# Threshold attention on one core: first keys rounded from PSUM, 20 exponential buffers, a new order table and one more GpSimd drain

## The chip, the core and the metric

The kernel runs on one core of one Trainium2 chip. The metric is the device time of one execution in microseconds (us), the median of several runs. Five engines work in their own instruction queues: TensorE (PE: matmuls and transposes), VectorE (DVE), ScalarE (ACT), GpSimd (POOL) and SyncE (SP, which issues transfers). A matmul writes to PSUM, and here only ACT and DVE empty PSUM. "The granted clock" is TensorE's, as a share of full speed.

## What is computed

For each of 96 heads (batch 8 by 12 heads), with Q, K and V of 512 rows by 64 in float32:

```python
scores  = einsum('bhqd,bhkd->bhqk', Q, K) / 8
weights = softmax(scores)                      # over the keys
weights = where(weights > 0.1, weights, 0)
weights = weights / (sum(weights) + 1e-10)
out     = einsum('bhqk,bhkd->bhqd', weights, V)
```

With normally distributed inputs almost no softmax weight is over 0.1, so nearly all rows of the output are zero.

## The kernel before

It uses that. Approximate weights in fp16 are computed for everything, only to find the few rows of Q in which a weight may pass the threshold. Those rows are gathered, scored again in float32, and their results are scattered into an output that is filled with zeros meanwhile. A check at the end (line 769 loads one number, `many`) branches to an exact fallback, which isn't taken here.

**Tiling.** Two heads are a pair, two pairs a quad: 48 pairs in 24 quads. A pair's scores are made in 4 score steps of 128 keys, each for both heads, so there are 192 score steps and 384 exponentials of 128 by 512. Quads 0 and 1 are brought in by single pairs, so that work can start sooner.

**What is done for a quad.** `load_k` and `load_q` (lines 330, 334) bring K in two 128 KB transfers per pair, one for each head, and Q. `do_ktr` (381) transposes K on PE in float32 into two PSUM banks, half the keys in each. `do_kev` (389 on ACT, 391 on DVE) copies each bank to SBUF in float32 (`kt`, which the later rescoring reads). `do_kh` (396 on ACT, 400 on GpSimd) casts `kt` to fp16 for the scores. `do_qcast` (367, 371) casts Q to fp16, `do_qtr` transposes it, and `do_qev` (416) copies that to SBUF. `do_sc` (438) makes the scores of one step, in two PSUM banks. `do_ex` takes an exponential from one bank into an fp16 buffer `e`: ACT by its function (447), DVE by arithmetic on the number's bits (449). `do_sm` (468) sums them and their eighth powers over the keys on PE. `do_bits` (425 GpSimd, 427 ACT, 429 DVE) makes the squares, or on DVE a bound of them, of the fp16 keys and queries of a quad, in two steps (a = 0 queries, a = 1 keys), and `do_norms` (478) adds them up on PE in an accumulator of their own, 4 matmuls for a quad; the maximum of these norms (`do_nm`, 491) bounds the error of fp16 and goes into the check.

**The chain behind.** The pairs form three groups (24, 16 and 8 pairs). For a group, when its sums are complete: `y` (the threshold, 483 ff.), `d`, `fl`, `mx` (candidate rows). Then for each of 6 stages of 8 pairs: `m`, `ix`, `qi`, `qf` (row numbers; 513, 524, 529), `gq` (GpSimd gathers rows of Q, 534), `xm` and `xev` (547), `xqk` (rescoring in float32 on PE, 556), `xexp` (ACT, 562), `xcut`, `xkeep` (DVE, 566, 570), `vi`, `oi` (575, 580), `gv` (GpSimd gathers rows of V, 585) and `scatter` (GpSimd, 600). The last group has one stage, number 5. The output's zeros are 24 transfers of 512 KB on SP's queue (607).

**What sets the order.** Each of these steps is added to a plan with its dependencies and the buffers that it takes and gives back. A table `ORDER`, one word for a step, lists them all in one sequence: the word's digits (base 36) are the step's number, its letter the engine (P, V, A, G for PE, DVE, ACT, GpSimd; S and Q for loads issued by SP and by ACT; N for none). The steps are emitted in that sequence, and each engine works through its own in that order. Buffers come from rings, first freed first used: 7 PSUM banks (`one`), 32 SBUF buffers of 512 KB for loads, `kt`, fp16 operands and squares (`big`), 14 for exponentials (`e`). A load waits on its queue until the buffer that the sequence gives it is free. `behind` and `alone` keep certain GpSimd and DVE steps from running at once. Constants are steps too: `const_base` (23 short DVE instructions, up to line 265) is needed first by the index step `qi`.

## Time and profile before

| | |
|---|---|
| median of 3 runs | 174.43 us (173.22, 174.43, 174.43) |
| the profiled execution | 173.78 us |
| its span, first to last instruction | 172.0 us |
| PE busy | 160.1 us (93%), 2190 instructions |
| DVE busy | 150.1 us (87%), 349 |
| ACT busy | 149.4 us (87%), 297 |
| POOL (GpSimd) busy | 130.4 us (76%), 198 |
| mean granted clock | 0.994 |

Busy times are sums over the whole span; a busy PE is not PE at its peak, since its matmuls are pipelined and their ends are modelled. Idle time of an engine that nobody waits for costs nothing. The single rows read from the trace stand in a section of their own below.

### The profile page before, as it was taken

The numbers are of one execution on the slowest core, as the hardware profiler recorded it, in microseconds if no ns is written. First come the engines' busy times: TensorE is split into PE (matmuls) and PEld (weight loads), VectorE is DVE, ScalarE is ACT, GpSimd is POOL, SyncE is SP. The second block draws the span as 40 slices with busy tenths as digits, with TensorE's granted clock in tenths as the row PEclk, the third lists the DMA queues.
The fourth block names the chain that finished last, engine by engine and source line by source line (L and its number), as shares of the span: only waits on it lengthen the run. The fifth ranks groups of instructions, "written<-read, shape, count | busy, mean of one in ns | idle before, by whom it ended". The sixth has DMA issues, their size and how long they took to land. (4 is left out here: it accounts for less than half of the span.)

```text
span 172.0 us, 5811 instructions
## 1 busy us (share of the span) xinstructions
PE 160.1 (93%) x2190; PEld 62.7 (36%) x2190; DVE 150.1 (87%) x349; ACT 149.4 (87%) x297; POOL 130.4 (76%) x198
## 2 busy tenths in 40 slices
PE   6598999999999999999999999999999999998950
PEld 2253443443354243434442354334243333332320
DVE  5198999999999999999999999899689999997450
ACT  2577999999999999999999999999899999936720
POOL 8119979999989988960785999799869959536451
PEclk9999999999999999999999999999999999999997
DMA  5999999989899689796998989999899980000000
GB/s 162 263 234 286 238 268 252 278 194 270 184 269 289 143 235 379 166 326 150 226 331 243 320 185 264 360 385 266 268 308 374 398 346 13 1 3 5 6 5 7
DMA packets 67453, 38.27 MB, mean 222 GB/s; under 512 B 51938, under 2 KB 64349, under 8 KB 67424
## 3 DMA queue, kind: packets, MB, share of 16 engines
q1 hardware_dynamic: 64992, 37.10, 76.1%
q10 hardware_dynamic: 1856, 0.66, 1.6%
q8 instruction: 17, 0.28, 0.7%
q0 software_dynamic: 576, 0.13, 0.5%
q14 instruction: 12, 0.10, 0.2%
HBM read 25.56 MB, written 12.78 MB: 223 GB/s over the span
## 5 line engine op out<-in xcount | busy, mean ns | idle before, releaser
L447 ACT ACTIVATE e<-one 128x512 f16<-128x512 f32 x231 | 120.0, 639 | 3.2 <-PE one L438 2.2
L449 DVE TENSOR_SCALAR e<-one 128x512 uint16<-128x512 f32 x153 | 97.0, 683 | 3.3 <-PE one L438 2.9
L438 PE MATMUL one<-big 64*128 64x512 f16 x384 | 67.6, 391 | 1.0 <-ACT big L396 0.5
L468 PE MATMUL sum<-e,w_s 128*32 128x512 f16 (+1 forms) x768 | 59.4, 387 | 0.9 <-ACT e L447 0.7
L425 POOL TENSOR_TENSOR big<-big 128x512 bf16<-128x512 f16 x52 | 52.8, 1038 | 2.3 <-DVE big L429 1.8
L400 POOL CAST big<-big 128x512 f16<-128x512 f32 x47 | 28.2, 613 | 16.3 <-ACT big L389 4.5
L371 POOL CAST qh<-big 128x512 f16<-128x512 f32 x45 | 26.7, 614 | 6.0 <-DMA big<-in_Q_dram 3.0
L438 PEld LDWEIGHTS <-big 64*128 64x128 f16 x384 | 17.2, 97 | 34.5 <-issue 28.1
L468 PEld LDWEIGHTS <-w_s 128*32 128x32 f16 (+1 forms) x768 | 15.9, 95 | 36.1 <-issue 31.5
L389 ACT COPY big<-one 128x512 f32<-128x512 f32 (+1 forms) x37 | 20.5, 591 | 2.7 <-PE one L381 2.6
L416 DVE COPY big<-one 128x512 f16<-128x512 f16 (+1 forms) x52 | 19.5, 398 | 3.3 <-PE one L410 1.2
L381 PE MATMUL one<-identity_f,big 64*128 64x64 f32 x384 | 18.7, 234 | 1.7 <-DMA big<-in_K_dram 1.5
L381 PEld LDWEIGHTS one<-identity_f,big 64*128 64x128 f32 x384 | 16.1, 145 | 6.9 <-issue 3.0
L391 DVE COPY big<-one 128x512 f32<-128x512 f32 (+1 forms) x15 | 9.7, 649 | 3.6 <-PE one L381 3.4
L556 PE MATMUL one<-big,xq 128*32 128x512 f32 x96 | 11.5, 598 | 0.5 <-issue 0.5
L410 PEld LDWEIGHTS <-qh 64*128 64x128 f16 x384 | 9.0, 97 | 7.6 <-issue 3.5
L410 PE MATMUL one<-identity_h,qh 64*128 64x64 f16 x384 | 11.3, 195 | 0.0
L534 POOL DMA_INDIRECT qs<-in_Q_dram,idx x6 | 6.4, 1060 | 6.2 <-DVE idx L524 4.8
L600 POOL DMA_INDIRECT out_dram<-vr,idx x6 | 6.1, 1024 | 4.1 <-DVE cut L566 2.2
L427 ACT ACTIVATE big<-big 128x1024 bf16<-128x1024 f16 x8 | 8.3, 1059 | 0.0
L585 POOL DMA_INDIRECT vr<-in_V_dram,idx x6 | 6.4, 1066 | 2.3 <-DVE idx L575 1.3
L562 ACT ACTIVATE one<-one 128x512 f32<-128x512 f32 x6 | 3.7, 612 | 3.3 <-DVE vals L504 2.0
(83 smaller groups left out, 80.9 us busy)
## 6 DMA issues: line engine op xcount, KB each, us to landing
out_dram<-zero SPq DMA_DIRECT2D x24, 512.0 KB, 6.2
big<-in_K_dram SPq DMA_DIRECT2D x93, 128.0 KB, 4.2
big<-in_Q_dram SPq DMA_DIRECT2D x22, 512.0 KB, 5.5
big<-in_Q_dram SPq DMA_DIRECT2D x3, 256.0 KB
big<-in_K_dram ACTq DMA_DIRECT2D x3, 128.0 KB
big<-in_Q_dram ACTq DMA_DIRECT2D x1, 256.0 KB
qs<-in_Q_dram,idx POOLq DMA_INDIRECT x6
vr<-in_V_dram,idx POOLq DMA_INDIRECT x6, 4.0
```

Of the source, the lines that this page charges most:

```text
L371: behind(nc.gpsimd.tensor_copy(dst, src))
L381: nc.tensor.matmul(dst[i][:, c:c + D], lhsT=src[ps, n0 + n, r, :], rhs=identity_f32[ps, ps], is_transpose=True, start=True, stop=True)
L389: nc.scalar.copy(dst, src)
L400: behind(nc.gpsimd.tensor_copy(dst, src))
L410: nc.tensor.matmul(dst[i][:, c:c + D], lhsT=src[ps, n0 + n, r, :], rhs=identity_h[ps, ps], is_transpose=True, start=True, stop=True)
L416: nc.vector.tensor_copy(qk_b[big("qk", q)][:, 0, n0:n0 + k, i * SO * D:(i + 1) * SO * D], src)
L425: behind(nc.gpsimd.tensor_tensor(out=dst[:, n, :], in0=src[:, n, :], in1=src[:, n, :], op=ALU.mult))
L438: nc.tensor.matmul(one[at("one", ("sc", hp, t, h))][:], lhsT=qk[ps, 1, n, t * P:(t + 1) * P], rhs=qk[ps, 0, n, :], start=True, stop=True)
L447: nc.scalar.activation(dst, src, ACTF.Exp, scale=scale, bias=-11.0 * math.log(2.0))
L449: nc.vector.tensor_scalar(dst.bitcast(u16), src, scale * LOG2E * 1024.0, 4096.0, op0=ALU.mult, op1=ALU.add)
L468: nc.tensor.matmul(dst[32 * j:32 * j + 32, :], lhsT=w, rhs=x, start=first, stop=False, skip_group_check=True)
L556: nc.tensor.matmul(one[at("one", ("xs", x))][sl, :], lhsT=xq_b[at("xq", x)][:, n, sl], rhs=kt_b[big("kt", quads[j])][:, n, :], start=(n == ...
```

## The change

1. A new step `kx` for the first unit (pair 0, `units[0]`): each half of its transposed K is rounded from its PSUM bank straight to the fp16 operand, on ACT or DVE. `kh` of that pair is gone. The float32 copies (`kev`) are still made, after `kx` in each bank. The score steps of pair 0 wait only for the half that holds their 128 keys (`t // 2`).
2. The ring `e` has 20 buffers, not 14.
3. `ORDER` is a new table (1327 words, 1325 before), so all queues have a new order and many steps are on another engine.
4. One `nc.gpsimd.drain()` is added as a step behind the last group's `mx`; the last scatter comes after it.
5. In the branch that isn't taken, two loads go to ACT's queue.

```diff
-ORDER = """6N fQ hS 1G gQ 24S 7P 18Q 22S 8P 9P 0G 5V 23S ...
+ORDER = """0G fS hQ iV 6N 4G 7P 8P 9P aP bP cP dP gQ jP ...
-    pools = {"one": 7, "sum": 1, "big": 32, "qh": 2, "e": 14,
+    pools = {"one": 7, "sum": 1, "big": 32, "qh": 2, "e": 20,
...
+    def do_kx(eng, u, i):
+        q, n, _ = u
+        src = one[at("one", ("ktr", u, i))][:, 0:SO * D]
+        dst = qk_b[big("qk", q)][:, 1, n, i * SO * D:(i + 1) * SO * D]
+        if eng == "ACT":
+            nc.scalar.copy(dst, src)
+        else:
+            nc.vector.tensor_copy(dst, src)
...
+        split = u == units[0]
+        for i in range(2) if split else ():
+            add(("kx", u, i), {"ACT": 0.27, "DVE": 0.33}, 0.15, [("ktr", u)], g0 - 9,
+                lambda e, u=u, i=i: do_kx(e, u, i), takes=[("big", ("qk", q))] if i == 0 else [])
         for i in range(2):
             add(("kev", u, i), {"ACT": 0.055 + 0.207 * k, "DVE": 0.062 + 0.267 * k}, 0.15,
-                [("ktr", u)] + [("kev", w, 0) for w in prev] + [("kev", u, 0)] * i, g0 - 9,
+                [("ktr", u)] + [("kx", u, i)] * split + [("kev", w, 0) for w in prev] + [("kev", u, 0)] * i, g0 - 9,
...
-        for n in range(n0, n0 + k):
+        for n in range(n0, n0 + k) if not split else ():
...
-                add(("sc", hp, t), {"PE": 0.22}, 0.23, [("qev", u, 0), ("qev", u, 1), ("kh", q, n)], g - 3,
+                add(("sc", hp, t), {"PE": 0.22}, 0.23, [("qev", u, 0), ("qev", u, 1)] + ([("kx", u, t // 2)] if split else [("kh", q, n)]), g - 3,
...
-            xstep("scatter", {"POOL": 1.25}, 0.3, ["gv", "oi"] + [("z", j) for j in quads_of(x)], do_scatter)
+            xstep("scatter", {"POOL": 1.25}, 0.3, ["gv", "oi"] + [("z", j) for j in quads_of(x)]
+                  + [("drain", 0)] * (x == NX - 1), do_scatter)
+    add(("drain", 0), {"POOL": 1.95}, 0.0, [("mx", NG - 1)], 999, lambda e: nc.gpsimd.drain())
```

**What the new table moves, counted.** Steps on each engine up to its last exponential, and the squarings (bits) behind it:

| | ACT before | ACT now | DVE before | DVE now |
|---|---|---|---|---|
| exponentials | 231 | 238 | 153 | 146 |
| K evictions, full (two pairs) | 31 | 28 | 13 | 16 |
| K evictions, half (one pair) | 6 | 3 | 2 | 5 |
| `kx` | - | 2 | - | 0 |
| `kh` casts | 1 | 2 | 0 | 0 |
| `qcast` casts | 2 | 0 | 1 | 1 |
| `y` | 1 | 0 | 1 | 2 |
| index steps `qi`, `qf` | - | - | 7 | 10 |
| `const_base` | - | - | at the very start | at about the 211th exponential |
| bits | 2 | 0 | 9 | 4 |
| bits behind the last exponential | 6 | 8 | 5 | 15 |

DVE's cast of Q is that of quad 1's second pair before, and of the very first pair now, ahead of all other work on data. GpSimd has 21 bit steps (26 before), 45 casts of K (47), 47 of Q (45), and the drain, which stands behind the last `gq` and ahead of the last three `gv`. `const_base` stands behind work of the full stretch now.

**The loads at the start.** Before, ACT's queue had both head halves of K of pair 0, Q of pair 1 and one half of K of pair 1, and SP's had Q of pair 0, Q of quad 1's first pair, then the rest. Now SP issues the first half of K of pair 0, then K of quad 1's first pair, its Q, K of pair 1 and the others; ACT issues Q of pair 0 and then the second half of K of pair 0.

**The loads late in the order.** The K of quad 20 now takes a buffer that the first rescoring (stage 0) gives back, 10 score steps ahead of its transposes, and the four transfers of K of quad 21 stand just ahead of it on SP's queue. Q of quad 12 has a buffer that comes free 10 score steps ahead too (by the casts of quad 11). In the old table the shortest such distance was 8 score steps (K of quad 17), and the next 16 and more.

ACT's queue at its start, before: names are buffers (`big` the large ring, `qh` the cast of Q, `one` a PSUM bank, `e` an exponential).

```order
L330 DMA big0_114<-in_K_dram 128x4x64 x2
L334 DMA big1_115<-in_Q_dram 128x2x256
L330 DMA big0_114<-in_K_dram 128x4x64
L367 ACT_TABLE_LOAD
L367 CAST qh0_146<-big1_115 128x512
L389 COPY big4_118<-one1_107 128x256
L396 CAST big5_119<-big4_118 128x512
L367 CAST qh1_147<-big2_116 128x512
L447 ACTIVATE e1_149<-one1_107 128x512
```

And the same place now, where the lines 407 and 456 are `kx` and the exponential:

```order
L334 DMA big1_115<-in_Q_dram 128x2x256
L330 DMA big0_114<-in_K_dram 128x4x64
L407 ACT_TABLE_LOAD
L407 CAST big2_116<-one1_107 128x256
L407 CAST big2_116<-one2_108 128x256
L456 ACTIVATE e0_148<-one6_112 128x512
L456 ACTIVATE e0_148<-one5_111 128x512
L456 ACTIVATE e1_149<-one3_109 128x512
```

Two of four load issues, two casts of Q, the half eviction and the cast behind it have left ACT's head; the two halves of K come from the PSUM banks `one1` and `one2`, and exponentials follow at once.

ACT's queue from its last exponential on, before (427 squarings, 547 `xev`, 562 the exponential of the rescoring):

```order
L447 ACTIVATE e8_156<-one0_106 128x512
L427 ACTIVATE big10_124<-big16_130 128x1024
L547 COPY xq1_187<-one1_107 128x256
L562 ACTIVATE one3_109,cut3_191<-one3_109 128x512
L547 COPY xq0_186<-one6_112 128x256
L427 ACTIVATE big7_121<-big29_143 128x1024 x2
L547 COPY xq1_187<-one3_109 128x256
L562 ACTIVATE one1_107,cut4_192<-one1_107 128x512
L427 ACTIVATE big24_138<-big4_118 128x1024
L562 ACTIVATE one6_112,cut5_193<-one6_112 128x512
L427 ACTIVATE big17_131<-big6_120 128x1024
L427 ACTIVATE big21_135<-big2_116 128x1024
```

And now, from behind the first rescoring of the tail on (436 squarings, 556 `xev`, 571 the exponential of the rescoring):

```order
L571 ACTIVATE one6_112,cut3_197<-one6_112 128x512
L436 ACTIVATE big10_124<-big13_127 128x1024
L571 ACTIVATE one1_107,cut4_198<-one1_107 128x512
L556 COPY xq1_193<-one4_110 128x256
L571 ACTIVATE one5_111,cut5_199<-one5_111 128x512
L436 ACTIVATE big29_143<-big16_130 128x1024
L436 ACTIVATE big4_118<-big30_144 128x1024
L436 ACTIVATE big28_142<-big26_140 128x1024
L436 ACTIVATE big11_125<-big0_114 128x1024
L436 ACTIVATE big9_123<-big1_115 128x1024
```

Five squarings now stand behind the last rescoring exponential (`cut5`), where two stood.

DVE's queue behind the rescoring exponential of stage 4, before (429 bits, 566 `xcut`, 570 `xkeep`, 575 `vi`):

```order
L429 TENSOR_SCALAR big24_138<-big4_118 128x512
L566 TENSOR_SCALAR cut4_192<-cut4_192 128x1
L570 SCALAR_TENSOR_TENSOR junk_200,accs_98<-one1_107,cut4_192,key_no_93 128x512
L575 TENSOR_SCALAR idx4_178<-accs_98,base_96 128x1
L566 TENSOR_SCALAR cut5_193<-cut5_193 128x1
L570 SCALAR_TENSOR_TENSOR junk_200,accs_98<-one6_112,cut5_193,key_no_93 128x512
L575 TENSOR_SCALAR idx5_179<-accs_98,base_96 128x1
```

And now (438 bits, 575 `xcut`, 579 `xkeep`, 584 `vi`):

```order
L575 TENSOR_SCALAR cut4_198<-cut4_198 128x1
L579 SCALAR_TENSOR_TENSOR junk_206,accs_98<-one1_107,cut4_198,key_no_93 128x512
L584 TENSOR_SCALAR idx4_184<-accs_98,base_96 128x1
L438 TENSOR_SCALAR big29_143<-big16_130 128x512
L438 TENSOR_SCALAR big23_137<-big17_131 128x512 x2
L438 TENSOR_SCALAR big4_118<-big30_144 128x512
L438 TENSOR_SCALAR big25_139<-big12_126 128x512 x2
L575 TENSOR_SCALAR cut5_199<-cut5_199 128x1
L579 SCALAR_TENSOR_TENSOR junk_206,accs_98<-one5_111,cut5_199,key_no_93 128x512
L584 TENSOR_SCALAR idx5_185<-accs_98,base_96 128x1
```

Six bit steps now stand between the index of stage 4's V rows and the cut of stage 5.

## Rows read from the trace of the kernel before

**Rows 1.** Stretches: from:to, length, busy us PE, PEld, DVE, ACT, POOL, clock, DMA, GB/s.

```profile
7.00:20.00 13.00, 11.62 (x119) 5.01 (x113) 11.34 (x25) 10.49 (x23) 7.94 (x15) 1.00 1.17 253
20.00:130.00 110.00, 109.56 (x1612) 43.30 (x1612) 104.46 (x208) 107.69 (x218) 93.22 (x146) 1.00 0.94 263
130.00:151.22 21.22, 20.81 (x288) 7.44 (x282) 20.75 (x39) 20.96 (x42) 16.52 (x19) 1.00 0.55 211
151.22:168.54 17.32, 14.18 (x150) 5.25 (x142) 11.02 (x38) 8.36 (x15) 9.29 (x9) 1.00 0.03 5
168.54:172.00 3.46, 0.00 (x0) 0.00 (x0) 0.00 (x0) 0.00 (x0) 0.00 (x0) 0.70 0.04 9
```

**Rows 2.** Instructions by line and form: count, busy us, mean ns, idle before.

```profile
L447 ACT ACTIVATE e<-one 128x512 f16<-128x512 f32 x231 | 120.0, 639 | 3.2 <-PE one L438 2.2 <-PE sum L468 0.4
L449 DVE TENSOR_SCALAR e<-one 128x512 uint16<-128x512 f32 x153 | 97.0, 683 | 3.3 <-PE one L438 2.9
L389 ACT COPY big<-one 128x512 f32<-128x512 f32 x31 | 18.5, 632 | 0.1
L391 DVE COPY big<-one 128x512 f32<-128x512 f32 x13 | 8.9, 684 | 0.2
L427 ACT ACTIVATE big<-big 128x1024 bf16<-128x1024 f16 x8 | 8.3, 1059 | 0.0
L429 DVE TENSOR_SCALAR big<-big 128x512 int32<-128x512 int32 x14 | 6.1, 451 | 0.0
L389 ACT COPY big<-one 128x256 f32<-128x256 f32 x6 | 2.1, 379 | 2.6 <-PE one L381 2.6
L391 DVE COPY big<-one 128x256 f32<-128x256 f32 x2 | 0.8, 420 | 3.4 <-PE one L381 3.4
```

**Rows 3.** Timeline of the head: start us, length us, engine, instruction, wait before.

```profile
0.75 1.32 ACTq L330 DMA_DIRECT2D big<-in_K_dram  x2
...
1.61 3.18 PE L340 MATMUL one<-blank,w_n 128*32 128x512 bf16 x28 [1.61 <-DVE w_n L210]
...
2.03 0.15 DVE L260 TENSOR_SCALAR base<-slot_i 128x1 f32<-128x1 int32 x1
...
3.30 0.28 DVE L265 TENSOR_SCALAR is_row<-slot_i 128x1 f32<-128x1 int32 x3
...
6.28 0.69 PE L381 MATMUL one<-identity_f,big 64*128 64x64 f32 x8 [1.49 <-DMA big<-in_K_dram]
...
7.34 0.48 DVE L416 COPY big<-one 128x256 f16<-128x256 f16 x2
7.52 0.62 ACT L396 CAST big<-big 128x512 f16<-128x512 f32 x1 [0.18 <-DVE big L391]
...
8.20 1.97 PE L438 MATMUL one<-big 64*128 64x512 f16 x8 [0.47 <-ACT big L396]
```

**Rows 4.** Timeline of the tail, the same columns.

```profile
152.53 0.22 DVE L524 TENSOR_SCALAR idx<-one,base 128x1 int32<-128x1 f32 x1
...
162.54 1.99 ACT L427 ACTIVATE big<-big 128x1024 bf16<-128x1024 f16 x2
...
165.12 0.81 PE L478 MATMUL one<-big,w 128*32 128x512 bf16 x10
...
167.11 0.69 DVE L491 TENSOR_REDUCE nmax<-one 128x1 f32<-128x512 f32 x1 [1.76 <-PE one L478]
167.55 0.99 POOL L600 DMA_INDIRECT out_dram<-vr,idx  x1 [0.91 <-issue]
...
168.29 0.16 DVE L768 TENSOR_REDUCE many_f<-one 1x1 f32<-1x11 f32 x1 [0.29 <-PE one L766]
```

**Rows 5.** The page's DMA issues: count, KB each, median us from issue to landing.

```profile
big<-in_K_dram SPq DMA_DIRECT2D x93, 128.0 KB, 4.2
```

**Rows 6.** Instructions of the program's end: ns min/median/max, first to last start.

```profile
L841 POOLq DRAIN  x3: 45/107/1611, 169.5 to 171.7; - x3
L841 SPq DRAIN  x3: 7/7/13, 170.6 to 171.4; - x3
```

14 lines of the change are left out of this document (8 added, 6 removed).

## The prediction

> **What bounds the kernel now.** I read the busy time by stretches first [rows 1]. From 20 to 130 us ScalarE (ACT) is busy 107.69 of 110 us and VectorE (DVE) 104.46; from 130 to 151.22, where the last exponential ends, 20.96 and 20.75 of 21.22. TensorE (PE) looks full too, but its matmuls overlap in the record, and the two engines that empty PSUM are what has no room left: the middle is their work, shared out by the table. The granted clock is 1.00, the upper level of 2.4 GHz, until 168.54, so it plays no part. At the two ends nothing is full. From 7 to 20 us ACT lacks 2.51 of 13 us and DVE 1.66. In the tail, 151.22 to 168.54, ACT works 8.36 and DVE 11.02 of 17.32 us: a chain of steps (threshold, gather, rescoring, gather, scatter) runs beside leftover squarings and norms. Then 3.46 us follow in which no counted instruction runs. So a microsecond of work taken from one of the two engines in the middle is worth half a microsecond, one taken from a chain at either end a whole one, and one of GpSimd's (93.22 of 110) nothing.
>
> The sum is made against the profiled execution: 173.78 us, a span of 172.0 and 1.78 around it. That is 0.65 under the median of 174.43. One per cent, about what a measurement of this kernel can tell from no change, is 1.74 us.
>
> **The middle.** The prices are the busy time of a group over its count [rows 2]: an exponential 0.519 us on ACT and 0.634 on DVE; a full K eviction 0.597 and 0.685, a half one 0.35 and 0.40; the two bit steps 1.04 and 0.436. A cast, or the threshold step y, I price as a full copy of its engine. Counted up to the last exponential (the table of counts with the change), ACT gets 7 exponentials (+3.63), two half copies straight to fp16 (+0.70) and one cast (+0.60), and loses three full and three half evictions (-1.79, -1.05), two bit steps (-2.08), y (-0.60) and one cast of Q (-0.60; the other that it loses lay in the wait for the first K): -1.2. DVE loses 7 exponentials (-4.44), five bit steps (-2.18) and a cast (-0.69), and gets three full and three half evictions (+2.05, +1.20), y (+0.69), three index steps (+0.66, at the 0.22 of [rows 4]) and the constants of line 250, which were free: they ran from 2.03 to 3.58 us, before any data had come [rows 3], and now stand in the middle of the full stretch (+1.55): -1.2 again. Both engines lose the same, so the middle shortens by **1.2 us** however the idle time falls. Prices by whole durations instead of shares would make it 1.6, average pitches 0.8. The five bit steps that GpSimd loses cost and save nothing while it has 15% to spare.
>
> The idle time that is left between 20 and 151.22 us is 2.57 us on ACT and 6.01 on DVE [rows 1], a mean of 4.3. Twenty exponential buffers and the new order could fill some; a tighter queue of loads could add some. Bounds: half of it filled (-2.1), or stalls added as below. I take 0, since in rows 1 neither engine waits long anywhere and nothing shows that 14 buffers held the tensor engine back.
>
> **The head.** The first scores start at 8.20 us, right behind the fp16 cast on ACT (7.52 to 8.14), though the evictions of Q had ended at 7.82 [rows 3]. With both halves rounded straight from PSUM that cast is gone, and Q's evictions end last: -0.32. The fp32 evictions are still made, but behind, on DVE, where nothing waits for them until the rescoring. Ahead of that, the K transposes began at 6.28, ended by a wait of 1.49 for a K load. Now the two K halves come first on SP and second on ACT, and the 256 KB of Q of quad 1, which SP issued second, comes behind three more K loads. How much sooner K lands no row tells: nothing at worst, and at best the transposes follow the warm-up matmuls, which end at 4.79 (-1.49). I take the middle, -0.75. Rule and row pull apart here: in the Trainium skill, "DMA: Bandwidth & Descriptors", section "Issuing engines are not separate DMA queues", loads started from several engines run on the same DMA engines and interleave, and a second issuer saves issue time alone. By it K would land as late as before; that is the second rival. Behind the first scores, of the mean idle time of 2.1 us from 7 to 20 us [rows 1] I let a quarter go, -0.5 (bounds 0 and -2.1). Head: **-1.6 us**.
>
> **The tail.** This is where I expect time back. The squarings left out of the middle stand behind the last exponential now. On DVE ten more of them (0.436 each) lie between the short steps; of those, the six ahead of the last cut fill a wait for ACT and may run over it by some 0.5 us, on the chain of the scatters. On ACT it is clearer. Before, two bit steps followed the third rescoring exponential (162.54, 1.99 us for both [rows 4]) and ended at 164.53. Now five follow it: three more at 1.0, ending near 167.5. The last norm sums on PE need them: four sets of four matmuls follow the last bit step, and by 10 matmuls in 0.81 us they take 1.3, so the maximum of the norms (line 491), which began at 167.11, cannot begin before 168.8: +1.7. Before, this step began 1.18 us after PE's record ended (165.93 to 167.11); matmul ends are modelled, PE then had a queue of sets to work off, and now it has nearly none, so I leave that out, but keep it as the upper bound, +2.9. The chain up to the third exponential gets 0.22 shorter, because an index step at 152.53 leaves the threshold chain. After the maximum come check, matmul, reduction (end 168.45) and the branch, and 3.55 us to the end of the span. The last scatter ended its issue at 168.54, level with the check; 0.5 us later it would still be hidden behind a check that is 1.5 later. Tail: **+1.6 us** after rounding, bounds +1.0 and +2.7.
>
> **The drain.** The longest GpSimd drain is 1.61 us from 169.5 on, behind everything [rows 6]; its like in mid-tail is the price of the new one. It stands between the last Q gather and the first V gather of the last three, on a queue that then has about a microsecond of slack; behind it wait three gathers and three scatters. SP's own drain comes 1.1 us after the GpSimd one starts, so at most 0.5 us can be saved at the end if the early drain empties the late one. I take 0, bounds -0.5 and +0.5. Two K and Q loads moved to SP's queue: each holds it 0.66 us [rows 3], in the first five microseconds, where transfers and not issues end the waits.
>
> Sum: -1.2 - 1.6 + 1.6 + 0 = -1.2, so 173.78 - 1.2 = **172.6 us**.
>
> **Rivals.** *The idle time is filled as well.* If the deeper buffers and the new order take half of the 4.3 us, the time is 172.6 - 2.1 = 170.5. For it: both engines' shares are 95 to 98%, so the rest is many short waits, of the kind that looser order removes. Against: the same many waits had no common cause in rows 1. *The head stays.* K lands as late as before and the idle time from 7 to 20 us stays; only the 0.32 of the cast is gained: 173.78 - 0.32 - 1.2 + 1.6 = 173.9. *Slower: loads come late.* PE runs in order, and a K transpose whose load is not there stops everything behind it. In the new table the K of quad 20 goes into a buffer that the first rescoring frees, ten score steps ahead of its use, and K of quad 21 is issued in front of it. With 384 exponentials in 143 us, ten steps are 7.4 us; eight K issues at 0.66 and a landing of 4.2 [rows 5] are 9.5. That is 2.1 us of stall; Q of quad 12 has ten steps too. Before, only one load had so few (eight, for one quad's K). One such stall of 1.2 us eats the gain; both at 2.1 give 176.8. Against: the landing time is a median under a full queue, and a queue that has just waited is empty.
>
> **How the numbers follow.** The sum as made 0.47 (its own range 171.5 to 173.7), idle time filled too 0.20, head unchanged 0.18, late loads 0.15. The range takes the first three and half of the last: 169.9 to 175.3. Faster by over 1% is under 172.69: all of the second case and somewhat over half of the first, 0.46; slower is over 176.17: most of the last, 0.13; the rest, 0.41, is the same.
>
> **What would show it.** The first scores near 7.1 us; ACT's and DVE's last exponentials near 148.4 with 7 exponentials moved; five bit steps in a row on ACT behind the third rescoring exponential, and the norms' maximum over 17 us after the last exponential (15.9 before). Transposes of K waiting for a load near 105 us would show the slower rival; a first K transpose still at 6.3 the second. I am wrong if the last exponential comes over 2 us off 148.4, or if the tail from there to the end stays at 20.8 us.

## The result, and the profile after the change

| | before | changed |
|---|---|---|
| median of 17 executions | 173.84 us (172.78 to 174.80) | 175.30 us (174.17 to 177.11) |
| ratio, 95% interval | | 1.0082 [1.0058, 1.0105] |
| profiled execution | 173.78 us | 175.38 us |
| its span | 172.0 us | 173.6 us |

A gain of 1.2 us was forecast, and the kernel became 1.5 us slower: less than the 1% that was set as the bound of "the same", but a loss beyond the interval, and the sign is the other one. The two profiled executions differ by 1.6 us, so their traces can be read against each other term by term. Ratios, here and below, leave out the executions over 1.5% above their kernel's fastest; two of the traces below, that of the first repeat and that of the kernel without three scatters on chip 9, are of such executions.

The stretches of the changed kernel, cut at the same events as [rows 1]: from and to, length, busy us of PE, PEld, DVE, ACT and POOL, granted clock, DMA share, GB/s.

```profile
7.00:20.00 13.00, 12.19 (x164) 5.76 (x162) 11.59 (x27) 11.81 (x25) 8.74 (x14) 1.00 0.92 229
20.00:130.00 110.00, 109.00 (x1588) 43.47 (x1587) 104.88 (x226) 107.08 (x218) 85.09 (x129) 1.00 0.96 262
130.00:149.23 19.23, 18.80 (x261) 6.89 (x260) 17.41 (x37) 18.30 (x38) 14.91 (x19) 1.00 0.65 261
149.23:170.54 21.31, 14.53 (x140) 5.35 (x138) 13.74 (x45) 10.32 (x17) 9.28 (x9) 1.00 0.02 4
170.54:173.60 3.06, 0.00 (x0) 0.00 (x0) 0.00 (x1) 0.00 (x0) 0.00 (x0) 1.00 0.04 11
```

The last exponential ends at 149.23 instead of 151.22, two microseconds sooner. The stretch from there to the check has grown from 17.32 to 21.31, four microseconds: that is where all of the loss lies. (The clock of 1.00 in the first line covers only the time that is on record, from 10.09 us on; see "The clock" below.) Between 20 us and the last exponential ACT idles 3.85 us (129.23 less 107.08 and 18.30) and DVE 6.94, against 2.57 and 6.01 before.

The head, as in [rows 3]: start, length, engine, instruction, and the wait before it.

```profile
5.57 0.69 PE L381 MATMUL one<-identity_f,big 64*128 64x64 f32 x8 [0.78 <-DMA big<-in_K_dram]
...
6.26 0.65 ACT L407 CAST big<-one 128x256 f16<-128x256 f32 x2 [3.08 <-PE one L381]
...
7.02 1.03 PE L447 MATMUL one<-big 64*128 64x512 f16 x4
```

K's transposes begin at 5.57 (6.28 before), the two new casts run straight behind them, and the first scores start at 7.02 (8.20 before).

The end of the middle and the tail, as in [rows 4]. Lines 543, 594 and 609 are the gathers of Q, of V and the scatters, 477 the sums, 497 the threshold step `y`, 571 the rescoring exponential, 500 the norms' maximum.

```profile
146.37 1.00 POOL L543 DMA_INDIRECT qs<-in_Q_dram,idx  x1 [0.45 <-DVE e L458]
146.50 0.60 PE L447 MATMUL one<-big 64*128 64x512 f16 x4
...
147.67 1.02 POOL L609 DMA_INDIRECT out_dram<-vr,idx  x1 [0.30 <-issue]
147.80 1.09 ACT L456 ACTIVATE e<-one 128x512 f16<-128x512 f32 x2 [0.93 <-PE one L447]
147.84 1.39 DVE L458 TENSOR_SCALAR e<-one 128x512 uint16<-128x512 f32 x2 [1.01 <-PE one L447]
148.45 1.23 PE L477 MATMUL sum<-e,w_s 128*32 128x512 f16 x12 [0.37 <-issue]
...
149.00 1.00 POOL L609 DMA_INDIRECT out_dram<-vr,idx  x1 [0.30 <-issue]
...
150.31 0.98 POOL L609 DMA_INDIRECT out_dram<-vr,idx  x1 [0.30 <-issue]
...
152.33 0.68 DVE L497 TENSOR_SCALAR y<-sum 64x512 f32<-64x512 f32 x1 [2.76 <-PE one L550]
...
162.60 0.58 ACT L571 ACTIVATE one<-one 128x512 f32<-128x512 f32 x1 [2.04 <-PE one L565]
163.19 4.83 ACT L436 ACTIVATE big<-big 128x1024 bf16<-128x1024 f16 x5
...
168.60 1.01 POOL L609 DMA_INDIRECT out_dram<-vr,idx  x1 [0.92 <-DMA vr<-in_V_dram,idx]
169.20 0.69 DVE L500 TENSOR_REDUCE nmax<-one 128x1 f32<-128x512 f32 x1 [3.30 <-PE one L487]
170.38 0.16 DVE L785 TENSOR_REDUCE many_f<-one 1x1 f32<-1x11 f32 x1 [0.29 <-PE one L783]
```

Two things stand out. `y` needs the last sums, and PE's record of them ends at 149.68, yet `y` starts at 152.33, while three scatters run in a row from 147.67 to 151.29. And at 147.8 ACT and DVE both wait about a microsecond for scores that PE's record ends at 147.10, while a gather runs to 147.37. The five squarings in a row (163.19 to 168.02) are there as drawn, and the maximum follows. It starts on time: its norms' record ends at 169.11, within the scatter from 168.60 to 169.61, so not every matmul that ends beside such a transfer is late.

The difference between the two spans, by the events of the prediction:

| from | before | after | difference | forecast |
|---|---|---|---|---|
| start to the first scores | 8.20 | 7.02 | -1.18 | -1.07 |
| to the last exponential's end | 143.02 | 142.21 | -0.81 | -1.70 |
| to `y` | 0.60 | 3.10 | **+2.50** | 0 |
| to the third rescoring exponential | 10.14 | 10.27 | +0.13 | -0.22 |
| to the norms' maximum | 5.15 | 6.60 | +1.45 | +1.7 |
| to the end of `many` | 1.34 | 1.34 | 0 | 0 |
| to the span's end | 3.55 | 3.06 | -0.49 | 0 |
| sum | 172.0 | 173.6 | +1.6 | -1.2 |

(The forecasts of the tail add to 1.48; the prediction rounded them to 1.6.) One line that was not in the sum at all, the start of `y`, is worth 2.5 of the 2.8 us between forecast and result.

### The profile page after: what moved, and what is told of

Its sections match the earlier page's. It is cut to its first block, busy times and chain, and to the rows that moved or that the text cites. A ratio compares the mean times of both kernels' runs of the same rounds, so it can differ in the third digit from the quotient of the medians.

```text
span 173.6 us, 5814 instructions
## 1 busy us (share of the span) xinstructions
PE 159.1 (92%) x2190; PEld 63.3 (36%) x2190; DVE 149.6 (86%) x354; ACT 149.4 (86%) x298; POOL 120.7 (70%) x188
## 4 chain that ended last, share of the span: by engine, by line
PE 49%; ACT 20%; issue 8%; DMA 8%; SPq 6%; POOL 5%; DVE 1%; ACTq 0%; POOLq 0%; DVEq 0%
PE one L447 19%; ACT e L456 15%; PE sum L477 14%; SPq L616 5%; PE one L381 5%; PE one L565 4%; DMA out_dram<-zero 4%; PE one L419 2%; DMA big<-in_K_dram 2%; ACT big L436 2%; ACT big L389 2%; POOL big L434 2%; DMA qs<-in_Q_dram,idx 2%; PE one L487 1%; PE one L550 1%
## 5 line engine op out<-in xcount | busy, mean ns | idle before, releaser
L456 ACT ACTIVATE e<-one 128x512 f16<-128x512 f32 x238 | 122.2, 641 | 4.6 <-PE one L447 4.3
L458 DVE TENSOR_SCALAR e<-one 128x512 uint16<-128x512 f32 x146 | 92.5, 682 | 5.0 <-PE one L447 4.2
L434 POOL TENSOR_TENSOR big<-big 128x512 bf16<-128x512 f16 x42 | 42.7, 1048 | 1.6 <-DVE big L425 1.5
L400 POOL CAST big<-big 128x512 f16<-128x512 f32 x45 | 26.7, 616 | 20.9 <-DVE big L391 9.0
L371 POOL CAST qh<-big 128x512 f16<-128x512 f32 x47 | 27.7, 618 | 11.2 <-DMA big<-in_Q_dram 6.5
L425 DVE COPY big<-one 128x512 f16<-128x512 f16 (+1 forms) x52 | 18.4, 396 | 4.8 <-PE one L419 3.8
L381 PE MATMUL one<-identity_f,big 64*128 64x64 f32 x384 | 17.3, 229 | 0.8 <-DMA big<-in_K_dram 0.8
L389 ACT COPY big<-one 128x512 f32<-128x512 f32 (+1 forms) x31 | 17.1, 600 | 0.0
L391 DVE COPY big<-one 128x512 f32<-128x512 f32 (+1 forms) x21 | 12.6, 618 | 0.0
L487 PE MATMUL one<-big,w 128*32 128x512 bf16 x58 | 7.0, 382 | 2.7 <-ACT big L436 2.2
```

The lines of the kernel that those rows point to most:

```text
L371: behind(nc.gpsimd.tensor_copy(dst, src))
L381: nc.tensor.matmul(dst[i][:, c:c + D], lhsT=src[ps, n0 + n, r, :], rhs=identity_f32[ps, ps], is_transpose=True, start=True, stop=True)
L389: nc.scalar.copy(dst, src)
L400: behind(nc.gpsimd.tensor_copy(dst, src))
L425: nc.vector.tensor_copy(qk_b[big("qk", q)][:, 0, n0:n0 + k, i * SO * D:(i + 1) * SO * D], src)
L434: behind(nc.gpsimd.tensor_tensor(out=dst[:, n, :], in0=src[:, n, :], in1=src[:, n, :], op=ALU.mult))
```

## The experiments

**The theories.** *A:* while GpSimd runs its indirect transfers (gathers and scatters), the end of a matmul reaches the engines that wait for it late, and the new table puts three scatters beside the last sums. *B:* the `xm` matmuls, which now stand right behind the sums on PE, are what `y` waits for. *C:* PE has a backlog that its modelled ends do not show. *D:* the chip differs, not the order. *E:* the new order as a whole.

The trace of before already held a small case of A. Columns as above:

```profile
107.59 0.39 PE L438 MATMUL one<-big 64*128 64x512 f16 x2
...
107.62 1.06 POOL L534 DMA_INDIRECT qs<-in_Q_dram,idx  x1
...
108.89 0.60 ACT L447 ACTIVATE e<-one 128x512 f16<-128x512 f32 x1 [0.38 <-PE sum L468]
```

The exponential starts 1.30 us after its scores, where 0.42 to 0.45 is the median (start to start, over the traces), just behind the end of the gather at 108.68. The trace also holds the times at which the semaphore of TensorE was raised, from which the views infer who ended a wait. It was raised at 107.61 and then not until 108.80, 108.83, 108.86 and 108.90, though matmuls that raise it end on record from 107.69 on. So it is the signal that comes late here, and not the engine that waits for it.

In most of the experiments one number is followed: the **lag**, from the end of DVE's last exponential to the start of `y` (0.60 before, 3.10 in the changed kernel). Ratios are to the kernel before on the same chip. The moves in the table are made by a few lines behind `seq = self.simple()`, which take a step out and put it behind another (each run's MOVES are written short below):

```python
for what, eng, behind in MOVES:
    i = self.ids[what]
    seq = [w for w in seq if w[0] != i]
    seq.insert([w[0] for w in seq].index(self.ids[behind]) + 1, (i, eng))
```

### First comparison (chip 8)

*The changed kernel without the scatters of stages 0 to 2.*

```diff
 def do_scatter(e, x=x):
+    if x < 3: return
```

> The changed kernel without the scatters of stages 0 to 2 (their rows of the output stay zero); all else in place. In the changed kernel the threshold step y of the last group starts at 152.33 us, 3.1 us behind the end of the last exponential (149.23), where the kernel before needed 0.6. Theory A: a matmul's completion reaches the engines that wait for it only when GpSimd's indirect DMA instruction that runs then is over; three scatters stood in a row there (147.67 to 151.29). Then y starts about 0.7 us behind the last exponential, near 149.9, and the time falls by 2.0 to 2.6 us, to about 172.9. Theory B: the float32 selection matmuls (xm) of stages 3 and 4, right behind the last sums on TensorE, hold the completion back; then y stays 3.1 us behind and the time stays within 0.4 us of 175.3. Theory C: TensorE is simply behind with its sums; as B.

*The changed kernel with `xm` and the rescoring of stages 3 and 4 behind the index step of stage 5.*

```diff
+MOVES = (xm 3 behind ix 5), (xev 3 behind xm 3), (xqk 3), (xexp 3), (xm 4 behind xqk 3), (xev 4)
```

> The changed kernel with xm of stages 3 and 4, and what hangs on them (xev, xqk, xexp of stage 3), moved behind the index matmul of stage 5; the three scatters stay. Theory A (scatters hold the signal): y stays about 3 us behind the last exponential, and the time stays, or grows by up to 1 us as the rescoring of stage 3 now comes later. Theory B (xm holds it): y starts about 0.7 us behind, and the threshold chain and with it the time gain about 2.4 us. Theory C (a backlog of sums): y comes a little sooner at most, as the sums themselves are as many.

*The kernel before with two scatters brought to the last sums.*

```diff
+MOVES = (scatter 1 behind gq 3), (scatter 2 behind scatter 1)
```

> The kernel before with the scatters of stages 1 and 2 moved right behind the Q gather of stage 3, so that they run at about 151.0 to 153.3 us, when the last sums (start 151.39) complete; nothing else moved. Theory A: y, at 151.82 in the kernel before, starts only when the scatters end, 153.5 or later, and the time grows by 1.2 to 2.0 us. Theory B or C: y stays within 0.3 us of 0.6 us behind the last exponential; the Q gather of stage 4 goes from 153.0 to 153.6, and the time stays within 0.5 us.

*The changed kernel without the new drain.*

```diff
-    add(("drain", 0), ..., lambda e: nc.gpsimd.drain())
+    add(("drain", 0), ..., lambda e: None)
```

> The changed kernel with the drain step left empty. In the changed kernel the drain takes 3.6 us (156.3 to 159.9), and the V gather of stage 3 waits behind it; the drain at the program's end takes 0.61 us where it took 1.61. If the check at the end (the norms' maximum) sets the end, the scatters come 2 us sooner for nothing, the drain at the end grows back by 1 us, of which up to 0.5 shows: the time grows by 0 to 0.5 us. If the scatters set the end, it falls by 1 us or more.

| | ratio | lag | last exponential to the norms' maximum |
|---|---|---|---|
| without three scatters | 0.9869 [0.9813, 0.9924] | 0.53 | 17.0 |
| `xm` later | 1.0139 [1.0078, 1.0200] | 0.53 | |
| before, with scatters | 1.0048 [1.0011, 1.0085] | 0.60 | |
| without the drain | 0.9887 [0.9813, 0.9961] | 0.54 | 17.0 |

By itself the first line is what A expected. The last line takes that away: there all three scatters run, and `y` does not wait. The kernel without the drain:

```profile
147.73 1.70 PE L477 MATMUL sum<-e,w_s 128*32 128x512 f16 x28
148.36 1.03 POOL L609 DMA_INDIRECT out_dram<-vr,idx  x1 [0.31 <-issue]
149.48 0.68 DVE L497 TENSOR_SCALAR y<-sum 64x512 f32<-64x512 f32 x1 [0.20 <-PE sum L477]
149.69 1.00 POOL L609 DMA_INDIRECT out_dram<-vr,idx  x1 [0.30 <-issue]
```

`y` starts 0.05 us after the sums, in front of two scatters, so the program holds no dependency of `y` on them. Either the drain makes the difference, though it stands further back in GpSimd's queue (at 156.3 us in the changed kernel), or the chip does. In the four traces of this chip no engine that waited for a matmul starts more than 0.25 us behind the matmul's recorded end. Before with the scatters is 0.5% slower without any lag. In its trace the last scatter ends at 167.66, just ahead of GpSimd's drain at the program's end, which then takes 3.22 us where it took 1.61. Moving `xm` costs the rescoring its early start (the third exponential at 161.22) and tells nothing of B here, as there is no lag to take away; but this kernel has the drain and all three scatters, and its 0.53 speaks for the chip.

### The changed kernel again (chips 9 and 2), and single terms (chip 9)

Four of the runs are the changed kernel unaltered, each beside others on its chip, to see how much of the lag comes again.

> The changed kernel as it is, for its trace a second time and its time on the same chip as the next two. In its first trace the threshold step y started 3.1 us behind the last exponential (the completion of the last sums came 3.0 us after their start). In three kernels that leave out the early scatters, the drain, or move xm, it started 0.53 behind. If the late completion belongs to the changed kernel's order, it is there again, 2.5 to 3.5 us; if it is an accident of single executions, y is at 0.5 to 0.7 here, and the norms' maximum 17.0 us behind the last exponential, not 19.97.

> The same kernel once more, for a third trace of it: as the run before. Also how far the last exponential's end varies from trace to trace: 149.23 us in the first, and 146.4 and 148.9 in kernels whose order up to it is the same.

> The changed kernel once more, on one chip with the next three. So far its late completion (the threshold step y 3.1 to 3.75 us behind the last exponential) stood in five of five traces of its order, taken on other chips than the three kernels without it (0.53: no early scatters, xm moved, no drain). Theory D: the chip makes the difference, and the drain, the scatters and xm none; then y has the same lag in all four kernels of this job, late or early. Theory E: it belongs to the order; then it is late here, 3 us or more, and early in the next three.

> The changed kernel, for the comparison on one chip with the next three. In all traces of chip 9 a completion of TensorE came up to 3.7 us late while GpSimd's indirect DMAs ran, in the four of chip 8 it never did. If this chip does it, y is 3.1 to 3.8 us behind the last exponential and the time 0.5 to 1.2% over the kernel before; if it doesn't, y is 0.5 behind, the span is some 2.5 us shorter, and the time is 0.5 to 1.5% under the kernel before.

| | ratio | lag | granted clock behind `y` |
|---|---|---|---|
| first repeat (chip 9) | 1.0043 [1.0011, 1.0075] | 3.16 | 0.5 from 153.4 to 156.8 |
| second (chip 9, one execution) | | 3.75 | 1.00 |
| third (chip 9) | 1.0099 [1.0049, 1.0149] | 3.73 | 0.5 from 152.8 to 156.2 |
| fourth (chip 2) | 1.0060 [1.0018, 1.0102] | 3.14 | 0.5 from 153.6 to 160.4 |

The lag is in every one, on two chips, and the loss in all three timed ones. `y` starts each time 0.6 to 1.1 us behind the last of the three scatters. The fourth repeat:

```profile
148.15 1.00 PE L477 MATMUL sum<-e,w_s 128*32 128x512 f16 x11 [0.20 <-DVE e L458]
...
150.21 0.98 POOL L609 DMA_INDIRECT out_dram<-vr,idx  x1 [0.30 <-issue]
...
151.84 0.68 DVE L497 TENSOR_SCALAR y<-sum 64x512 f32<-64x512 f32 x1 [2.81 <-PE one L550]
```

*The constants ahead again*, which the sum had charged DVE with 1.55 us:

```diff
+MOVES = (const 1, POOL, behind const 4), (const 5, DVE, behind const 1)
```

> The changed kernel with the constants of the index steps (const_rows on GpSimd, const_base on VectorE) back at the start, where both engines wait for the first loads; 1.55 us of VectorE's work leave the full stretch. By the sum of the prediction half of it counts, since the two engines share the exponentials: 0.8 us less. If ScalarE alone sets the pace (its share of the stretch 97%, VectorE's 95%), nothing: within 0.3.

Measured: 1.0082 [1.0040, 1.0124], lag 3.72; from the first score to the last exponential 141.4 us, where the changed kernel's own traces show 141.3 to 143.1. The 0.8 us cannot be seen; a term of that size is smaller than what the middle varies by from trace to trace.

*Five squarings moved from behind the third rescoring exponential to ACT's waits ahead of it:*

```diff
+MOVES = (bits 11 and 14, a = 0, behind bits 19, a = 1), (bits 10 behind xexp 4), (bits 21 and 18 behind xev 5), all ACT
```

> The changed kernel with the five squarings that stand on ScalarE behind the last rescoring exponential moved into its waits ahead of that (two behind the squarings of quad 19, one behind the fourth rescoring exponential, two behind the last xev). In the trace they run 163.19 to 168.02, and the norms' maximum is at 169.20. If they set the end, the maximum comes some 3 us sooner; then the last scatter (ends 169.61) and the load of the check's number behind it on GpSimd set the end, and the time falls by 0.7 to 1.0 us. If the scatters set the end already, no change.

Measured: 1.0010 [0.9973, 1.0048], against 1.0043 for the changed kernel in the same comparison; lag 3.74. The maximum came 19.4 us after the last exponential, and was itself late: 1.53 us behind the end of its norms, beside a scatter from 165.84 to 166.87. The squarings may be worth about half a microsecond as long as the wait for `y` stands in front; the two intervals overlap, so this is not shown.

### The same pairs on one chip (chip 9)

The kernels of the first comparison that mattered, again without the drain, without the three scatters, and with `xm` later, beside the third repeat.

> The changed kernel without the drain, again, beside the changed kernel itself. Its program differs from that one by one instruction on GpSimd alone. Theory D: y as late as in the changed kernel here, and the time within 0.6 us of it. Theory E: y 0.5 us behind the last exponential, and the time some 2.5 us under the changed kernel's.

> The changed kernel without the scatters of stages 0 to 2, whose rows stay zero, again. Theory A (scatters hold the completion while they run): y 0.5 us behind the last exponential whatever the chip does with the others, and the time 2.5 to 4 us under the changed kernel's. Theory D: y as late as in the others.

> The changed kernel with xm of stages 3 and 4 and what hangs on them behind the index matmul of stage 5, again. Theory B (xm right behind the last sums holds their completion while the scatters run): y 0.5 us behind the last exponential here while the changed kernel's is late. Theory D: as late as in the others of this job. Theory A: late, if the changed kernel's is late.

| | ratio | lag | maximum behind the last exponential |
|---|---|---|---|
| changed (third repeat) | 1.0099 [1.0049, 1.0149] | 3.73 | |
| without the drain | 1.0177 [1.0092, 1.0262] | 3.76 | |
| without three scatters | 0.9873 [0.9816, 0.9931] | 0.50 | 17.5 |
| `xm` later (one execution: 179.15 us) | | 3.77 | |

The kernel without the drain, the same that did not wait on chip 8:

```profile
146.78 1.84 PE L477 MATMUL sum<-e,w_s 128*32 128x512 f16 x28
...
150.05 0.98 POOL L609 DMA_INDIRECT out_dram<-vr,idx  x1 [0.30 <-issue]
151.93 0.68 DVE L497 TENSOR_SCALAR y<-sum 64x512 f32<-64x512 f32 x1 [3.25 <-remote]
```

the kernel without the three scatters:

```profile
148.12 1.81 PE L477 MATMUL sum<-e,w_s 128*32 128x512 f16 x28
149.97 0.68 DVE L497 TENSOR_SCALAR y<-sum 64x512 f32<-64x512 f32 x1 [0.16 <-PE sum L477]
```

and the kernel with `xm` later, where line 540 is the first matmul that needs the outcome of `y`:

```profile
146.81 1.92 PE L489 MATMUL sum<-e,w_s 128*32 128x512 f16 x28
...
152.04 0.69 DVE L509 TENSOR_SCALAR y<-sum 64x512 f32<-64x512 f32 x1 [3.27 <-remote]
...
155.28 0.58 PE L540 MATMUL one<-ones,m 64*128 64x1 f32 x2 [6.34 <-DVE m L534]
```

PE's work is the same in the first two, 28 matmuls of sums recorded in 1.8 us. With the scatters `y` starts 3.31 us after them, without 0.04. So the drain is not the cause. Nor is `xm` (B: moved away, the lag is 3.77), nor a backlog of PE (C: the same PE queue gives no lag without the scatters, and in the last kernel PE has nothing to do for 6.34 us, while `y` still waits 3.27). The scatters are, on this chip: A stands. And the chip decides whether it happens (D): without the drain the same kernel gave 0.9887 on chip 8 and 1.0177 on chip 9, with `xm` later the lag was 0.53 and 3.77, and without the three scatters the two chips agree, at 0.9869 and 0.9873. The signals that go the other way are on time: in the 14 traces with late completions, PE starts within 0.06 us of the end of the ACT or DVE instruction that it waits for in all 29 waits of over 0.2 us that end beside a gather or scatter.

### Scatters into before, scatters out of the changed kernel (chip 2)

*Before with two scatters at the last sums, again; and the changed kernel without the drain with its three scatters behind the V gathers of stages 3, 4 and 5, alone and with the five squarings moved:*

```diff
+MOVES = (scatter 0 behind gv 3), (scatter 1 behind gv 4), (scatter 2 behind gv 5)
```

> The kernel before with the scatters of stages 1 and 2 moved behind the Q gather of stage 3, beside its last sums, again, since the chip of the first try showed no late completions at all. On a chip with late completions theory A wants y 2.5 us or more behind the last exponential (0.6 in the kernel before), and the time 1 to 2 us over the kernel before; on a chip without, the time within 0.6% of it, as in the first try.

> The changed kernel without the drain, and with the scatters of stages 0, 1 and 2 moved into waits of GpSimd: behind the V gathers of stages 3, 4 and 5. Nothing is left out. Theory A (on a chip with late completions the three scatters beside the last sums cost 2.5 to 3 us): y is 0.5 to 0.7 us behind the last exponential here too, the norms' maximum 17 to 18 behind it, and the time 1.5 to 2.5 us under the changed kernel's. If the lateness is of the place, not of the scatters: y stays 3 us behind, no gain. On a chip without late completions: within 1 us of the changed kernel.

> The kernel before this one, and the five squarings behind the last rescoring exponential moved into ScalarE's waits, as tried alone already. The norms' maximum then needs only the last rescoring exponential's successors on VectorE; the chain of the last V gather and scatter should set the end. A further 0.3 to 1.0 us less, so 1 to 2% under the kernel before.

| | ratio | lag | maximum behind the last exponential |
|---|---|---|---|
| changed (fourth repeat) | 1.0060 [1.0018, 1.0102] | 3.14 | |
| before, with scatters | 1.0072 [1.0042, 1.0103] | 2.01 | |
| scatters later | 0.9971 [0.9930, 1.0012] | 0.49 | 18.0 |
| and squarings moved | 0.9992 [0.9954, 1.0030] | 0.50 | 17.3 |

The kernel before with two scatters beside its last sums:

```profile
149.28 1.48 PE L476 MATMUL sum<-e,w_s 128*32 128x512 f16 x24
150.04 1.02 POOL L608 DMA_INDIRECT out_dram<-vr,idx  x1 [0.30 <-issue]
151.37 1.00 POOL L608 DMA_INDIRECT out_dram<-vr,idx  x1 [0.30 <-issue]
152.21 0.68 DVE L496 TENSOR_SCALAR y<-sum 64x512 f32<-64x512 f32 x1 [1.67 <-PE one L549]
```

This makes the lag in the old order, without the new table (E falls): 0.60 becomes 2.01. The kernel is 0.7% slower, but it was 0.5% slower on chip 8 without a lag, so the ratio alone would not have shown it. `y` starts ahead of the second scatter's end (152.37), so that a completion is held until all of them are over, as A had it, is too strong; that it is late beside them is what the row shows. The scatters taken out of the changed kernel's bad place, and the drain with them, give back 0.9%, by intervals that only just part. It is not all, since the scatters now stand beside the norms, whose maximum waits in turn. The kernel with later scatters:

```profile
164.90 0.60 PE L496 MATMUL one<-big,w_n 128*32 128x512 bf16 x6
164.97 1.01 POOL L618 DMA_INDIRECT out_dram<-vr,idx  x1 [0.31 <-issue]
...
166.69 0.69 DVE L509 TENSOR_REDUCE nmax<-one 128x1 f32<-128x512 f32 x1 [3.93 <-PE one L353]
```

The squarings moved as well bring nothing more: the maximum is held 2.20 us after the end of its norms.

### Scatters tied to `y` (chip 0)

*Without the drain, the scatter of stage 0 waits for `y` itself, that of stage 1 stands behind it, that of stage 2 behind the V gather of stage 3; alone and with the squarings moved:*

```diff
+        if x == 0:
+            tc.add_manual_dep(inst.ins, ys[-1].ins.name, ...)   # ys: the y instructions
+MOVES = (scatter 2 behind gv 3)
```

> The changed kernel without the drain, in which the scatters of stages 0 and 1 keep their place but wait until the last group's y has run, and that of stage 2 stands behind the V gather of stage 3. Theory A: y starts 0.5 to 0.7 us behind the last exponential on any chip, although the scatters run right after it; the norms' maximum follows 17 to 18 us behind the last exponential (19.97 in the changed kernel), and the time is 2 to 3 us under the changed kernel's (1.006 to 1.01 of before on chips with late completions): 0.988 to 0.998 of the kernel before. If not the scatters but the work of the place holds y, it stays 3 us late and the time at or over the kernel before.

> The same, and the five squarings that stand behind the last rescoring exponential moved into ScalarE's waits. Then neither squarings nor scatters should hold the norms' maximum: about 15.5 to 16.5 us behind the last exponential, and the last scatter near it; 0.3 to 1.2 us under the kernel beside it, 0.983 to 0.995 of the kernel before, which would beat both.

Measured: 171.10 us, 0.9904 [0.9871, 0.9937], and 170.88 us, 0.9907 [0.9870, 0.9943]. Both beat the kernel before on this chip. The maximum comes 17.06 and 15.2 us after the last exponential, so moving the squarings does bring it 1.9 us forward, but the end of the program hardly moves. With the squarings in their old place, the maximum and the drains of the program's end (here and below, a DRAIN row: count, ns min/median/max, first to last start):

```profile
164.39 0.69 DVE L507 TENSOR_REDUCE nmax<-one 128x1 f32<-128x512 f32 x1 [2.94 <-PE one L494]
```

```profile
L869 POOLq DRAIN  x3: 45/107/1610, 166.8 to 169.0; - x3
```

And with them moved:

```profile
161.82 0.69 DVE L512 TENSOR_REDUCE nmax<-one 128x1 f32<-128x512 f32 x1 [0.70 <-PE one L499]
...
163.77 1.01 POOL L621 DMA_INDIRECT out_dram<-vr,idx  x1 [0.89 <-DVE many_f L801]
```

```profile
L874 POOLq DRAIN  x3: 45/113/3099, 164.6 to 168.3; - x3
```

With the squarings moved the last scatter is behind the check, and the end drain lasts until 2.9 us after that scatter's record ends: another chain has become the end. What these two do not show is whether the tie to `y` cures the lag, since no trace of this chip has a late completion anywhere. They show that the changed order, without the drain and with these scatters moved, is worth 1% where nothing is late, and no more. Whether the tied kernel beats before on a chip like 9 or 2 stays open.

## Why the prediction was wrong, step by step

**The middle (-1.2, and -0.5 of idle time behind the first scores): the work was right, the idle time wrong.** From the first score to the last exponential 0.81 us were gained of 1.7, and the last exponential came at 149.23 where 148.4 was forecast. Even that was gained early. The hundredth exponential ends at 44.26 instead of 46.21, and from there to the last one it takes 104.97 us instead of 105.01. In this stretch the work fell as it was priced, by 1.19 us on ACT (102.58 to 101.39) and 1.51 on DVE (99.79 to 98.28). But the idle time grew by as much, from 2.43 to 3.58 us on ACT and from 5.22 to 6.69 on DVE, where 0 was taken: that is the step that failed here. The page puts the growth down to waits for scores (over the whole span, idle time ahead of exponentials that scores ended: 2.2 and now 4.3 us on ACT, 2.9 and 4.2 on DVE). The wait at 147.8, 0.93 on ACT and 1.01 on DVE beside a gather, is one of them, but late completions do not explain the growth: on chip 8, where none is seen, the idle time of the same stretch is 1.51 and 3.93 us in the old order (with two scatters moved) and 2.02 to 2.57 and 4.95 to 5.52 in three traces of the new one. What makes these waits longer stays open. The bounds, "stalls added as below", looked for stalls from loads. The deeper ring filled no idle time; the rival that it would is not seen.

**The head (-1.07 to the first scores): right, in part by luck.** K's transposes began 0.71 us sooner, where 0.75 was chosen as the middle between 0 and 1.49, and the first scores 1.18 sooner, where 1.07 was summed. Other executions differ by more than such an agreement: in the 17 traces of the new order the transposes begin at 4.92 to 5.66 us and the scores at 6.12 to 7.11, in the three of the old at 6.28 to 6.69 and 8.06 to 8.38. What the prediction drew from the rule of the Trainium skill, "DMA: Bandwidth & Descriptors", section "Issuing engines are not separate DMA queues", that K would land as late as before, did not come true, by the 6.28 and 5.57 of the two traces. But the order of the loads and their issuer were changed at once, so the rule itself is not tested. The idle time from 7 to 20 us fell by 1.32 us on ACT and 0.25 on DVE, a mean of 0.79, where 0.5 was taken; the clock had a part in that (below).

**The slower rival, late loads: did not happen.** The transposes of K waited for a load 0.8 us in the whole trace, the 0.78 of the head. The slower side came by a mechanism that was not among the rivals.

**The tail (+1.6): the mechanism named was right, and a step was missing in front of it.** The five squarings, the maximum behind them and its size are as worked out: +1.45 from the third rescoring exponential to the maximum, +1.7 forecast. On chip 8, where nothing is late, the maximum comes 17.0 us after the last exponential in two kernels of the changed order, and 15.89 + 1.6 gave 17.5; in the old order, with two scatters moved, it comes 15.5 us after it there. The step that failed, and cost the sign, is the first one of the tail: the tail was counted from the last exponential as if `y` followed at once, as before, with only the instructions on DVE, ACT and PE between. In its place the runs showed a wait of 3.10 us, 2.50 more than before. The three scatters that the table had moved on GpSimd's queue to just ahead of that point were not looked at, because GpSimd was held to be free ("one of GpSimd's nothing"). That sentence of the prediction is the wrong one. GpSimd's time is not the bound, but when its indirect transfers run is a term of its own.

The sign was in the rows. The prediction saw that the maximum began 1.18 us after PE's record ended, said that PE then had a backlog, and left it out. The timeline of before has one row more at that place, which was not read:

```profile
165.63 1.01 POOL L600 DMA_INDIRECT out_dram<-vr,idx  x1 [0.41 <-DVE bad L758]
```

The norms end at 165.93 and the maximum starts at 167.11 [rows 4], and a scatter runs across the gap, to 166.64. That it was this and not a backlog, two later traces of the old order (with two scatters moved) show. They have the same norms and a scatter beside them: on chip 8 the norms end at 165.28 and the maximum starts at 165.34, on chip 2 at 166.33 and 167.49. With GpSimd's order laid beside it, the three scatters at the last sums might have been priced at about a microsecond each, an estimate from this one row.

**The drain (0, bounds -0.5 and +0.5): at its lower bound.** The new drain and those of the end of the changed kernel:

```profile
L760 POOLq DRAIN  x1: 3599/3599/3599, 156.3 to 156.3; - x1
...
L858 POOLq DRAIN  x3: 51/107/612, 171.6 to 173.3; - x3
```

It lasts 3.6 us, over twice the 1.61 of [rows 6] that was taken for it, and empties the one at the end: 0.61 instead of 1.61. Of that, 0.49 reaches the span's end (3.06 instead of 3.55), and every trace with the drain shows 3.05 to 3.09, those without it 3.54 to 3.60, or 5.16 to 5.23 where the last scatter ends just ahead of the end drain or behind its start. In the tail it holds the first V gather up:

```profile
160.99 1.02 POOL L594 DMA_INDIRECT vr<-in_V_dram,idx  x1 [3.39 <-DVE junk L579]
```

That gather's row numbers are there at 158.47, and in the kernels of the new order without the drain it follows them by 0.28 us at most. The 2.2 us that the drain costs it are hidden, as the last scatter still ends at 169.61, ahead of the end of `many` at 170.54.

**The clock plays no part: wrong at the start, and in some runs in the tail.** The record of the granted clock begins at 16.29 us in the trace of before and at 10.09 in that of the changed kernel, and the views count what lies ahead of it as 1.00. The matmuls tell more. In the trace of before, the 18 of the scores up to 16.2 us take 0.606 us each and the 38 from 16.3 to 30 us 0.386. In the kernel before with two scatters on chip 8, the record shows 0.50 from 8.20 to 15.00 us, and there, too, they take 0.606. So the clock was at its lower level, 1.2 GHz, until about 16 us before the change and about 10 us after it. In the three traces of the old order the slow score matmuls last to 14.4 us or longer; in the 17 of the new one to 12.6 at most, and ten have none. What it is worth, two traces of the changed kernel on chip 9 show: the first repeat has slow scores up to 12.1 us and ends its 48th exponential at 27.64, the second has none and ends it at 25.86. So part of the 1.95 us gained up to the hundredth exponential is the clock's. The sum had no term for it, and no run tested whether the new order brings it about.

In the tail of the profiled execution the record shows 1.00 to the end. In five of the other traces with the long wait (three of the four repeats, without the drain, `xm` later) the granted clock is at 0.5, the level of 1.2 GHz, for 3.4 to 6.8 us soon behind it. The fourth repeat and the second, from the last exponential to `y` and from there to the end of the rescoring:

```profile
148.70:151.84 3.14, 1.68 (x19) 0.60 (x14) 0.33 (x2) 0.28 (x1) 2.19 (x2) 1.00 0.03 5
151.84:164.40 12.56, 10.90 (x74) 2.87 (x75) 9.76 (x31) 5.03 (x12) 3.33 (x3) 0.73 0.01 3
```

```profile
148.46:152.21 3.75, 2.13 (x20) 0.87 (x15) 0.49 (x2) 0.82 (x1) 2.23 (x3) 1.00 0.03 4
152.21:163.40 11.19, 7.90 (x74) 2.36 (x75) 10.02 (x32) 5.11 (x12) 3.17 (x3) 1.00 0.02 3
```

The same 74 matmuls take 10.90 us of PE at a mean clock of 0.73 and 7.90 at 1.00, and the stretch, cut by the same steps, 12.56 instead of 11.19. PE had been busy 1.68 of 3.14 us in the wait ahead of the drop, and 2.13 of 3.75 where none followed; what tips it these rows do not say. The kernel with `xm` later on chip 8 has no lag, but PE waits there as well, busy 0.17 us from 146.96 to 150.21, and the clock is at 0.5 from 151.28 to 154.69. So the drop follows waits of PE, whatever they are for; that it follows from them fits the order of events, and no run tested it alone.

**What stays open.** Why a completion is held, and why on chips 9 and 2 and not on 8 and 0. The Trainium skill says in "Perfetto Trace Analysis", section "Tensor Engine Instruction (MATMUL, LD_WEIGHTS)", that the recorded end of a matmul is estimated from its size and not observed. This case's rows agree with the page as far as they go, the same 28 matmuls being recorded in 1.84 us with a lag of 3.76 and in 1.81 with one of 0.50. So the recorded ends cannot say whether the sums themselves ended late or only the signal did. The semaphore's times say a little more. In the changed kernel it was raised at 148.52 and next at 152.30, 152.40 and 152.45, for the sums and two sets of `xm` that end on record at 149.68, 150.48 and 151.40; without the drain on chip 8 it was raised at 149.45, 150.25 and 150.68, within 0.03 us of the recorded ends. Three signals that belong 1.7 us apart came almost at once, and PE had begun the `xm` behind the sums at 149.83. That fits signals that were held better than sums that ended late; only that the signals were late is shown. What sets the late completions beside some transfers apart from those on time beside others stays open too. The kernel before is itself slower on the chips that have them (173.8 in the first comparison, 173.8 and 173.2 on chip 9, 173.9 on chip 2, against 172.6 on chip 8 and 172.5 on chip 0); whether for the same reason is not shown. The changed kernel itself did not run on a chip without the effect; the one without the drain did, at 0.9887, and by that the forecast of 0.993 would have held there. That is worked out, not measured.

## What to carry to other kernels

An engine with time to spare can still cost time by when it works: lay the order of GpSimd's gathers and scatters beside the points where a serial chain waits for a matmul, and put them elsewhere or tie them behind that point. A start that lags the start of its matmul by more than the usual 0.45 us is a term of the sum, and before it is put down to the model of PE's ends, the other queues' rows of that moment should be read. And a move that helps on one chip (0.989) can hurt on another (1.018), so a schedule should be compared on several.

## What was not expected of the hardware

- On chips 9 and 2, and in the two first traces, many (not all) matmul completions come late beside indirect transfers of GpSimd: by 0.7 us for the exponentials at 147.8 and 1.2 to 1.5 for the norms' maximum beside one gather or scatter, a lag of 2.0 us instead of 0.6 with two scatters, and of 3.1 to 3.8 with three in a row. It is the signal of TensorE's semaphore that comes late, and signals to TensorE are on time. On chips 8 and 0 no trace shows it, with the same instructions.
- A GpSimd drain behind indirect transfers lasts 3.1 to 3.7 us when the last is not over or only just (3.60 in mid-tail, 3.10 at the end of the last kernel), 1.61 when it ended a microsecond before, and shortens the next one.
- The granted clock fell to 0.5 behind a wait of 3 to 4 us in which PE had been busy about half of the time, in some executions of a kernel and not in others. At the start, the time at which it rises differs from one execution of the same kernel to the next (slow scores up to 12.1 us, and none), and moves the 48th exponential by 1.8 us.
